# A scan kernel's last readout gives its first region beside the chain and splits its outputs on chip, and the second layer's gate is made beside the last attention

## The chip, the core and the metric

One core of a Trainium2 chip runs the whole program as one launch. The metric is the device time of one execution in microseconds (us), median of the runs shown.

## What is computed

Four layers in a row. Layer 1 is an RWKV-7 mixer over 256 context and 512 latent tokens (width 1024, 16 heads of 64): a recurrence over the tokens in two directions, a group norm of its output, a bonus term, a gate and an output projection. Layer 2 is a differential attention, layers 3 and 4 are hybrid attention layers. The change touches the end of layer 1's scan and the modulation of layer 2. Cut to that, the reference is:

```python
mod  = silu(c) @ ada_w[i] + ada_b[i]              # 3 x 1024 columns: shift, scale, gate
shift, scale, gate = split(mod)
h    = rms_norm(x, norm_g[i]) * (1 + scale) + shift
o    = scan(forward) + scan(backward)             # layer 1, per head a 64x64 state
y    = ((o - mean) * rsqrt(var + eps)) * gn_g + gn_b
y    = (y + sum(r * kd * r_k) * v) * silu(g)      # readout
x    = x + gate * (y @ w_out)
```

Every layer has this residual with a gate of its own, so the last third of the 3072 columns of `mod` is needed only where a layer's output is added back.

## The kernel before

**The scan.** Sixteen heads are worked in four pairs of feature blocks `p` (128 features `f` = 2p + j each), and the 768 tokens in three regions `R` of 256 (region 0 is the context, 1 and 2 are the latents). `Scan.chain` (L689) runs 48 steps, 12 per pair, 64 tokens of both directions each: products `ps_c` (L733), a copy to `rhs` (L740), the product with the inverted block (L768), the copy to `xz` (L771), then `ps_z` and `ps_o` (L778, L791) and the new state (L786). Each step waits for the one before on PE, ACT and DVE in turn. The four steps of a pair's first third cover region 0 in both directions, so region 0 of the last pair is complete when ten of the twelve groups of steps are done; regions 1 and 2 end only with the last step.

**The readout.** `readout(p)` (L820) takes a pair's summed outputs `osum`, subtracts the mean by a product with a block of ones (`center`, L857: L860, L861, squares L863, variance L866), takes one inverse square root over the 24 columns of the three regions (`rsqrt_dve`, 13 small DVE instructions, L72 to L76), and then for each region spreads it (L880, transposed on PE at L883, applied at L884), applies gain and bias (L889), loads two tiles `vs` from DRAM for each `j` (L853; six buffers, so three loads of two are in flight), adds two of their parts on POOL (L854), makes the bonus product (L891), and finishes with three elementwise steps (L893 to L895). The result goes to DRAM, `E.Y` (L896). For the last pair only region 0 is centred before the chain's end; all the rest waits for it.

**What follows.** The output projection needs these results as two parts, `hi` (rounded, written by ACT) and `lo` (the difference, by DVE), in tiles `act`: one pair for each group of 256 tokens, that is, for each region. `load_y` (L1134) reads `E.Y` from DRAM into `w_raw` and splits it. The object `Dense` is opened while the chain still runs (`early`, L976): blocks 0 to 5 of groups 0 and 1 are loaded, and `begin` starts the first two output blocks on them, on the first six of eight blocks. After the scan `dense` (L1818) loads blocks 6 and 7 of groups 0 and 1 and all of group 2, and `out_layer` (L1182) goes through the output blocks: 24 products each (L1079), evicted times the gate into a `yo` tile (L1212) and added to the residual (L1213), whose tiles `q_lo` and `q_hi` are loaded at L1808 and L1810.

**The modulation.** `ada` (L426) makes `mod` in pieces of 128 columns: one load of 512 KB (L432), 8 products of two columns, which the trace counts as 16 passes (L85), a copy (L87), a transpose (L90) and the bias (L96). 32 pieces run beside the chain: the gate of layer 1 (8) and all of layer 2 (24). Their buffer `ada_s` is single there, so a piece's load starts when the products of the piece before are done.

**The last attention of layer 2.** `phase_4` (L1491) runs `attention(hp)` for four pairs of heads, with a side stream that `run_streams` weaves in by counts (`NSIDE`). For the last pair the side stream has the gates and four calls of `load_y`, which bring the three earlier pairs' outputs back from DRAM. These, and the next weights, share the two buffers of `w_raw`.

**What sets the order.** The streams are woven by the numbers of the tables (`PC`, `TA`, `NSIDE` and so on); a scheduler then places the instructions of each engine, and each engine and the SP queue, which issues all DMAs, works strictly in the order it was given.

Of the kernel before, what the change touches and what calls it, by code (L numbers as in the profile page):

```python
# [205 lines left out]
class Scan:  # L206
# [3 lines left out]
    def __init__(self, E):  # L210
        self.E, self.D, self.lb = E, {}, {}
        self.ready, self.time, self.inverted, self.prepped, self.done = -1, 0.0, 0, 0, 0
        self.pend = self.pb = self.ppb = self.hop = self.pt = self.lb0 = None
        self.dones = [0] * CH
        self.read = 0
        self.ng = 0

# [601 lines left out]
    def readout(self, p):  # L819
# [47 lines left out]
            V.tensor_scalar(vc[:, R * 8:R * 8 + 8], ps[:, 0:8], 64e-5, None, OP.add)  # L867
            yield 0

        yield from center(0)  # L870
        if last:
            yield lambda: self.done >= 12
        for R in (1, 2):
            yield from center(R)
        y = rsqrt_dve(E, pool, vc, 24)
        yield 0
        for R in range(3):
            o = D["o"][R][0]
            rb = wide("rb")
            A.copy(fl(rb).rearrange("p (b v) -> p b v", v=64), y[:, R * 8:R * 8 + 8].unsqueeze(2).to_broadcast([128, 8, 64]))  # L880
            ps = psum()
            for b in range(4):
                P.transpose(ps[:, b * 128:b * 128 + 128], fl(rb)[:, b * 128:b * 128 + 128], E.ident)  # L883
            V.tensor_tensor(fl(o), fl(o), ps, OP.mult)  # L884
            yield 0
            for j in range(2):
                f = 2 * p + j
                oj, rj, pj = o[:, j, :], rb[:, j, :], ps[:, j * 256:j * 256 + 256]
                A.activation(oj, oj, AF.Identity, scale=vec(E, "gn_g", f), bias=vec(E, "gn_b", f))  # L889
                vs = streams(R, j)  # L890
                P.matmul(pj, brk[j], vs[1][:, 0], start=True, stop=True)  # L891
                yield 0
                V.tensor_tensor(rj, vs[0][:, 0], pj, OP.mult)  # L893
                (V if last and j else G).tensor_tensor(oj, oj, rj, OP.add)
                (V if last and j else G).tensor_tensor(oj, oj, vs[0][:, 1], OP.mult)  # L895
                nc.sync.dma_start(E.Y[f][:, R * 256:R * 256 + 256], oj)  # L896
                yield 0

# [39 lines left out]
CH = 1  # L940
# [3 lines left out]
def scan(E, stack):  # L944
# [2 lines left out]
    right = dict(side="right", bufs=1, reuse_waits="tile")  # L947
    left = dict(bufs=1, reuse_waits="tile")
    S = Scan(E)
    ada = [(0, m) for m in range(16, 24)] + [(1, m) for m in range(24)]  # L950
    with ExitStack() as k, ExitStack() as t, ExitStack() as a:
        kp = S.kp = k.enter_context(tc.tile_pool(name="kp", **right))
        with ExitStack() as b:
# [22 lines left out]
        def early():  # L976
            yield lambda: S.done >= 10 and S.inverted >= 6
            a.close()
            pool = stack.enter_context(tc.tile_pool(name="dn", **left))
            D.append(Dense(E, pool, stack.enter_context(tc.tile_pool(name="dn_ps", space=PSUM, **left))))  # L980
            S.pt = t.enter_context(tc.tile_pool(name="tp", **left))
            D[0].W.split(0)
            yield lambda: S.read >= 3
            D[0].load_y(E.Y, 0, 6, 2)
            if BG:
                D[0].begin(range(6))

        S.weave([x for x in rest if x in streams] + [
            [S.time + a * TC / 2, 0, S.chain(a, (0, 1) if CH == 1 else (a,)), TC, None, PC] for a in range(CH)] + [
# [499 lines left out]
def phase_4(D, hg, Y):  # L1489
# [44 lines left out]
    def attention(hp):  # L1534
# [68 lines left out]
                steps.append(tuple((lambda f=f, h=h, qb=qb: f(h, qb)) for f in (a, b, c)))  # L1603
        yield from D.pipeline(steps)

    def side(hp):
        yield from next_gates.pop()
        if hp < 3:
# [3 lines left out]
                yield next(next_gates[0])  # L1612
        else:
            ys = T["y"] = [D.group(), D.group()]
            for f in (0, 4):
                for g in range(2):
                    D.load_y(Y, f, min(f + 4, 6), g + 1, g, ys)
                    yield 0

    for _ in kqv(0):  # L1620
# [14 lines left out]
CM = 0  # L1635
OB5 = 1
GS = 0
NSIDE = (28, 8, 26, 10)
PM = 500

PW, PT4, PT5, PN = 2, 1, 1, 1
# [155 lines left out]
def dense(E, D):  # L1797
    nc, tc = E.nc, E.tc
    with tc.tile_pool(name="dm", bufs=1, reuse_waits="tile") as pool, \
            tc.tile_pool(name="dm_ps", bufs=1, space=PSUM, reuse_waits="tile") as pp:  # L1800
        D.open(pool, pp)
        D.load_y(E.Y, 6, 8, 2)
        D.load_y(E.Y, 0, 8, 3, 2)
        ys = D.ys
        cx = [pool.tile([128, 1024], FT, name="q_lo", bufs=2) for _ in range(2)]
# [124 lines left out]
```

## Time and profile before

| | us |
|---|---|
| median of 3 runs | 2320.38 |
| lowest and highest of them | 2319.94, 2320.71 |
| the profiled execution | 2326.66 |
| its span in the trace | 2324.6 |
| PE busy in it | 2106.3 (91%) |

The profiled execution is 6.28 us longer than the median, and 2.06 us of it lie outside the span. PE is busy most of the time, but the share is an average over stages: what a change in one stage is worth is read there, in the chain of waits and the timeline. "Granted clock" is the share of TensorE's full speed that it was given in a stretch: 1.0 is 2.4 GHz, 0.5 is 1.2 GHz, and values between are a mixture.

### The profile page before, as it was taken

How to read it: one execution, taken by the hardware profiler on the slowest of the kernel's cores; microseconds unless marked ns; L12 is line 12 of the kernel's file. 1: busy time of each engine (PE TensorE's matmuls, PEld its weight loads, DVE VectorE, ACT ScalarE, POOL GpSimd, SP SyncE). 2: the span in 40 equal slices, each digit the busy share in tenths (PEclk: the TensorE clock that was granted, in tenths of full speed). 3: DMA queues.
4: the chain of work that ended last, by engine and by line, in shares of the span. 5: the costliest groups of instructions: out<-in, count | busy, mean ns of one | idle time of the engine just before them, and what ended most of it. 6: DMA issues, size and time to landing. Idle time of an engine off the chain costs nothing.

```text
span 2324.6 us, 49071 instructions
## 1 busy us (share of the span) xinstructions
PE 2106.3 (91%) x18920; PEld 1867.2 (80%) x18920; DVE 1567.2 (67%) x3937; ACT 1167.2 (50%) x2634; POOL 686.0 (30%) x993
## 2 busy tenths in 40 slices
PE   7999999986899988886989999997899998999989
PEld 3989899975776776664888898987788987888878
DVE  5478868986288877723487767864676674677673
ACT  4455456563255544331255565664455564466652
POOL 0133523433036262321222223323223232032321
PEclk9999999986998788887999999998999999999999
DMA  7467456347544333153321111121312222321132
GB/s 245 136 204 227 144 188 216 105 151 230 184 135 130 90 110 101 54 181 93 134 93 55 47 58 44 42 85 48 114 64 82 67 78 91 119 80 66 60 100 82
DMA packets 190713, 263.60 MB, mean 113 GB/s; under 512 B 16145, under 2 KB 137489, under 8 KB 190353
## 3 DMA queue, kind: packets, MB, share of 16 engines
q1 hardware_dynamic: 190480, 260.48, 34.9%
q8 instruction: 149, 2.44, 0.4%
q14 instruction: 84, 0.68, 0.1%
HBM read 197.24 MB, written 63.18 MB: 112 GB/s over the span
## 4 chain that ended last, share of the span: by engine, by line
PE 47%; DVE 13%; DMA 4%; ACT 3%; issue 3%; POOL 1%; SPq 1%; ACTq 0%; DVEq 0%; POOLq 0%
PE ps_pj L1079 26%; PE ps_s L1376 3%; PE ps_m L85 2%; PE ps_t L1759 2%; PE ps_b L579 1%; PE ps_t L1586 1%; PE ps_s L1079 1%; PE ps_t L1745 1%; DMA w_raw<-in_wd_dram 1%; PE ps_t L1346 1%; DMA w_raw<-att 1%; PE ps_t L1575 1%; DVE ut L657 1%; PE ps_o L744 1%; PE ps_c L733 1%
## 5 line engine op out<-in xcount | busy, mean ns | idle before, releaser
L1079 PE MATMUL ps_pj<-w_hi,act 128*128 128x256 f32 x3264 | 645.5, 292 | 17.9 <-ACT act L1459 4.6
L1079 PEld LDWEIGHTS ps_pj<-w_hi,act 128*128 128x128 f32 x3264 | 529.5, 195 | 31.0 <-ACT act L1459 6.7
L1079 PE MATMUL ps_pj<-w_lo,act 128*128 128x256 f32 x1632 | 470.8, 289 | 0.0
L1079 PEld LDWEIGHTS ps_pj<-w_lo,act 128*128 128x128 f32 x1632 | 319.1, 196 | 0.6 <-issue 0.2
L246 PE MATMUL ps_pj<-h,b_hi 128*128 128x384 f32 (+1 forms) x1216 | 316.6, 341 | 2.7 <-ACT gh L352 1.5
L246 PEld LDWEIGHTS ps_pj<-h,b_hi 128*128 128x128 f32 x1216 | 220.0, 193 | 8.6 <-ACT gh L352 2.7
L246 PE MATMUL ps_pj<-h,b_lo 128*128 128x384 f32 (+1 forms) x608 | 206.9, 341 | 0.3 <-DVE b_lo L190 0.3
L1058 ACT CAST w_hi<-w_raw 128x1024 fp32r<-128x1024 f32 x120 | 121.0, 1050 | 58.9 <-DMA w_raw<-in_wd_dram 28.4
L1060 DVE TENSOR_TENSOR w_lo<-w_raw,w_hi 128x1024 fp32r<-128x1024 f32 x90 | 122.7, 1371 | 41.0 <-ACT w_hi L1058 40.3
L1079 PE MATMUL ps_pj<-act,w_hi 128*128 128x256 f32 x768 | 146.2, 286 | 0.0
L1735 POOL TENSOR_SCALAR p<-p,r 128x128 f32<-128x128 f32 (+2 forms) x64 | 71.8, 1122 | 239.3 <-DVE r L1729 156.7
L1060 POOL TENSOR_TENSOR w_lo<-w_raw,w_hi 128x1024 fp32r<-128x1024 f32 x30 | 72.8, 2428 | 234.3 <-ACT w_hi L1058 234.3
L579 PE MATMUL ps_b<-al,bk 64*128 64x128 f32 x768 | 127.4, 309 | 12.2 <-DVE rbk L587 10.7
L579 PEld LDWEIGHTS ps_b<-al,bk 64*128 64x128 f32 x768 | 105.7, 208 | 33.9 <-issue 21.0
L1079 PEld LDWEIGHTS ps_pj<-act,w_hi 128*128 128x128 f32 x768 | 120.9, 191 | 0.4 <-issue 0.2
L246 PEld LDWEIGHTS ps_pj<-h,b_lo 128*128 128x128 f32 x608 | 117.1, 193 | 3.6 <-issue 1.3
L547 POOL TENSOR_TENSOR s<-bk,src 64x256 f32<-64x256 f32 x96 | 76.9, 801 | 126.8 <-DVE bk L544 114.3
L1079 PE MATMUL ps_pj<-act,w_lo 128*128 128x256 f32 x384 | 109.6, 286 | 0.0
L1302 POOL TENSOR_TENSOR hx<-hx,ctab 128x256 f32<-128x256 f32 x80 | 68.0, 870 | 139.7 <-DVE ht L1300 82.5
L1565 POOL TENSOR_TENSOR p<-p 128x768 f32<-128x768 f32 x32 | 61.1, 1908 | 155.2 <-ACT p L1564 95.2
L1376 PE MATMUL ps_s<-k_s,q_hi 128*128 128x256 f32 (+2 forms) x256 | 91.2, 365 | 15.3 <-ACT p L1555 5.7
L85 PE MATMUL ps_m<-ada_s,cs 128*2 128x128 f32 x512 | 76.7, 314 | 13.4 <-DMA ada_s<-in_ada_w_dram 11.8
(323 smaller groups left out, 4920.0 us busy)
## 6 DMA issues: line engine op xcount, KB each, us to landing
w_raw<-in_wd_dram SPq DMA_DIRECT2D x120, 512.0 KB, 4.4
b_raw<-in_blocks_dram SPq DMA_DIRECT2D x84, 256.0 KB, 3.0
src<-streams SPq DMA_DIRECT2D x48, 384.0 KB, 3.6
ada_s<-in_ada_w_dram SPq DMA_DIRECT2D x32, 512.0 KB, 4.4
vs<-streams SPq DMA_DIRECT2D x48, 256.0 KB, 3.4
ada_w<-in_ada_w_dram SPq DMA_DIRECT2D x8, 1024.0 KB, 11.2
lr<-lora SPq DMA_DIRECT2D x96, 64.0 KB, 3.0
streams<-k SPq DMA_DIRECT2D x32, 192.0 KB, 2.8
```

What stands on the lines that cost most here:

```text
L85: nc.tensor.matmul(ps[0:2, 0:128 * n], E.cs[:, kb, :], w(kb), start=(kb == 0), stop=(kb == 7))
L246: E.nc.tensor.matmul(ps[gi][:, :m], w[:, kb % 4, :], h[:, kb, :], start=(n[gi] == 1), stop=(n[gi] == 24))
L547: G.tensor_tensor(v3(rev(s))[a:a + 64], ut[a:a + 64, 1 if a == 0 else 0], v3(rev(r))[a:a + 64], OP.mult)
L579: P.matmul(pb[:, c, :], bk[q:e, c].rearrange("p s t -> p (s t)"), al[q:e, c, h:3:2 - h, :], start=True, stop=True, tile_position=(q, 0))
L1058: nc.scalar.copy(hi[:, a:a + 4], raw)
L1060: e.tensor_tensor(lo[:, a:a + 4], raw, hi[:, a:a + 4], OP.subtract)
L1079: E.nc.tensor.matmul(ps, a(kb), b(kb), start=(k == 0), stop=(k == 23))
L1302: G.tensor_tensor(w4(x), w4(x), cb, OP.mult)
L1376: P.matmul(ps, q[i][:, 2 * j + h, c], k[h][:, j, a:a + n], start=(i == 0), stop=(stop and i == 1))
L1565: G.tensor_tensor(ps_[0], ps_[0], ps_[1], OP.add)
L1735: G.tensor_scalar(t, t, r[:, h:h + 1], None, OP.mult)
L1759: P.matmul(ps[h * 64:h * 64 + 64, :128], v[:, kb, o:o + 64], pt[:, h, kb, :], start=(kb == 0), stop=(kb == nk - 1), tile_position=(0, h * 64))
```

## The change

Three things, in one diff. (a) The body of the last loop of `readout` becomes `give(R, y)`. For the last pair region 0 gets an inverse square root of its own over 8 columns and is given as soon as it is centred and `Dense` has its tiles, before the wait for the chain's end; the other two regions share one over 16. (b) For the last pair regions 0 and 1 are not written to DRAM: ACT rounds them into `hi` and DVE writes the difference into `lo`, straight in the tiles of the output projection. The load of blocks 6 and 7 of groups 0 and 1 goes; region 2 still goes through DRAM. (c) The last 8 of the 24 pieces of layer 2's modulation, its gate, leave the scan. `late_gate` makes them in the side stream of the last attention, two ahead of each `load_y`, with their 512 KB in a `w_raw` buffer and their products in the bank `ps_pj`; `NSIDE` for it goes from 8 to 16.

```diff
@@ Scan.__init__
-        self.dones = [0] * CH
+        self.dones, self.next = [0] * CH, None
@@ readout
-        yield from center(0)
-        if last:
-            yield lambda: self.done >= 12
-        for R in (1, 2):
-            yield from center(R)
-        y = rsqrt_dve(E, pool, vc, 24)
-        yield 0
-        for R in range(3):
+        def give(R, y):
             o = D["o"][R][0]
...
-                nc.sync.dma_start(E.Y[f][:, R * 256:R * 256 + 256], oj)
+                if last and R < 2:
+                    hi, lo = self.next.ys[R]
+                    A.copy(hi[:, f, :], oj)
+                    V.tensor_tensor(lo[:, f, :], oj, hi[:, f, :], OP.subtract)
+                else:
+                    nc.sync.dma_start(E.Y[f][:, R * 256:R * 256 + 256], oj)
                 yield 0
+
+        yield from center(0)
+        if last:
+            y = rsqrt_dve(E, pool, vc[:, 0:8], 8)
+            yield lambda: self.next is not None and len(self.next.ys) == 2
+            yield from give(0, y)
+            yield lambda: self.done >= 12
+        for R in (1, 2):
+            yield from center(R)
+        a = 8 if last else 0
+        y = rsqrt_dve(E, pool, vc[:, a:24], 24 - a)
+        yield 0
+        for R in range(a // 8, 3):
+            yield from give(R, y[:, R * 8 - a:R * 8 + 8 - a])
@@ scan
-    ada = [(0, m) for m in range(16, 24)] + [(1, m) for m in range(24)]
+    ada = [(0, m) for m in range(16, 24)] + [(1, m) for m in range(16)]
...
+            S.next = D[0]
@@ phase_4
+    def late_gate(m):
+
+        w = D.first.tile([128, 8, 128], FT, name="w_raw", bufs=2)
+        nc.sync.dma_start(w, E.i["ada_w"][1, m // 4][:, :, m % 4 * 128:m % 4 * 128 + 128])
+        ada_bias(E, 1, m, 1, ada_columns(E, pool, D.pj, lambda kb: w[:, kb, :], 1))
@@ side
-            for f in (0, 4):
-                for g in range(2):
-                    D.load_y(Y, f, min(f + 4, 6), g + 1, g, ys)
+            for m in range(16, 24):
+                late_gate(m)
+                yield 0
+                if m % 2:
+                    f, g = divmod((m - 16) // 2, 2)
+                    D.load_y(Y, 4 * f, min(4 * f + 4, 6), g + 1, g, ys)
                     yield 0
@@
-NSIDE = (28, 8, 26, 10)
+NSIDE = (28, 16, 26, 10)
@@ dense
-        D.load_y(E.Y, 6, 8, 2)
         D.load_y(E.Y, 0, 8, 3, 2)
```

In the changed file later lines have moved: 1079 is 1092, 883 is 876, 891 is 884, 1047 is 1060, 1147 is 1160, 1173 is 1186, 1376 is 1389, 1575 is 1588, 1586 is 1599 and 1598 is 1611 there.

PE from the chain's last step (`ps_z`/`ps_o`, `ps_c`) to the first output block behind it, before. L85 and L90 are the modulation's pieces, L860 the centring of regions 1 and 2.

```order
L768 MATMUL ps_c<-rhs,lb 64x64 x8
L791 MATMUL ps_o<-rbk,xz 64x64 x8
L85 MATMUL ps_m<-ada_s,cs 2x128 x8
L860 MATMUL ps_g<-osum,bd_102 128x512
L90 MATMUL ps_m<-ident,ada_r 128x2
L85 MATMUL ps_m<-ada_s,cs 2x128 x8
L90 MATMUL ps_m<-ident,ada_r 128x2
L85 MATMUL ps_m<-ada_s,cs 2x128 x8
L90 MATMUL ps_m<-ident,ada_r 128x2
L860 MATMUL ps_m<-osum,bd_102 128x512
```

The same place in the changed program (L876 transposes region 0's inverse root, L884 is its bonus product, L1092 the first output blocks).

```order
L876 MATMUL ps_m<-ident,rb 128x128 x4
L733 MATMUL ps_c<-xz,al 64x64
L744 MATMUL ps_o<-al,xz 64x64
L733 MATMUL ps_c<-xz,al 64x64 x7
L744 MATMUL ps_o<-al,xz 64x64 x7
L884 MATMUL ps_m<-vs,brk 128x256
L768 MATMUL ps_c<-rhs,lb 64x64 x8
L884 MATMUL ps_m<-vs,brk 128x256
L791 MATMUL ps_o<-rbk,xz 64x64 x8
L1092 MATMUL ps_pj<-w_hi,act 128x256
L860 MATMUL ps_v<-osum,bd_102 128x512
```

Region 0's products now stand between those of the last step, no piece of the modulation stands behind it, and the blocks 6 and 7 of the first two output blocks stand between the centring of regions 1 and 2.

The SP queue beside the last attention of layer 2, before (L1147 brings the attention's outputs back, L1047 the next layer's weights):

```order
L1147 DMA w_raw<-att_69 128x4x256 x2
L1828 DMA q_hi<-resid 128x1024 x2
L1666 DMA v<-memv 128x512
L1388 DMA att_69<-y 128x512
L1147 DMA w_raw<-att_69 128x2x256 x2
L1047 DMA w_raw<-in_wd_dram 128x1024 x4
```

And in the changed program:

```order
L1622 DMA w_raw<-in_ada_w_dram 128x8x128 x2
L1849 DMA q_hi<-resid 128x1024 x2
L1688 DMA v<-memv 128x512
L1160 DMA w_raw<-att_69 128x4x256
L1622 DMA w_raw<-in_ada_w_dram 128x8x128
L1401 DMA att_69<-y 128x512
L1622 DMA w_raw<-in_ada_w_dram 128x8x128
L1160 DMA w_raw<-att_69 128x4x256
L1622 DMA w_raw<-in_ada_w_dram 128x8x128 x2
L1160 DMA w_raw<-att_69 128x2x256
L1622 DMA w_raw<-in_ada_w_dram 128x8x128 x2
L1160 DMA w_raw<-att_69 128x2x256
```

Eight loads have come between the four, through the same two buffers, and the next layer's weights now stand behind all twelve.

PE in that attention, changed (L1389 scores, L1588 transposes of the probabilities, L1599 their products with the values, L1611 the last transposes of a head):

```order
L90 MATMUL ps_pj<-ident,ada_r 128x2
L1588 MATMUL ps_t<-ident,p 128x128 x3
L1599 MATMUL ps_t<-v,pt 128x128 x6
L85 MATMUL ps_pj<-w_raw,cs 2x128 x8
L1588 MATMUL ps_t<-ident,p 128x128 x3
L1389 MATMUL ps_s<-k_s,q_hi 128x512
```

Each of the eight pieces stands like this among the scores and transposes of one head and of the first half of the next; the first output blocks of layer 2 (L1092), which before stood among the second head's steps, now follow the eighth piece.

## Rows read from the trace of the kernel before

**Rows 1.** The page of the profiled execution: its span.
```profile
span 2324.6 us, 49071 instructions
```

**Rows 2.** Windows of three stretches: length, busy us by engine, granted clock, DMA share, GB/s.
```profile
981.00:1056.50 75.50, 63.35 (x952) 50.01 (x944) 22.47 (x45) 24.85 (x53) 17.30 (x21) 0.86 0.50 155
1056.50:1108.50 52.00, 27.83 (x117) 18.96 (x116) 16.93 (x48) 9.18 (x18) 7.22 (x9) 0.68 0.32 98
1545.00:1615.00 70.00, 54.23 (x338) 47.16 (x336) 42.20 (x126) 41.42 (x91) 19.25 (x11) 0.85 0.19 61
```

**Rows 3.** The same windows for line 85 alone: length, PE and PEld busy, clock, DMA.
```profile
981.00:1056.50 75.50, 8.94 (x64) 5.61 (x64) 0.86 0.50 155
1056.50:1108.50 52.00, 7.39 (x48) 4.52 (x48) 0.68 0.32 98
```

**Rows 4.** Chain of waits around the end of the scan: start us, us, what ended last.
```profile
1052.53 4.22 DMA ada_s<-in_ada_w_dram
...
1065.08 4.06 DMA ada_s<-in_ada_w_dram
...
1108.47 16.64 PE ps_pj L1079 x122
```

**Rows 5.** Timeline at the last steps of the chain: start, us, instruction, idle and releaser.
```profile
1030.41 0.37 ACT L740 COPY rhs<-ps_c 128x256 f32<-128x256 f32 x1 [3.83 <-PE ps_c L733]
...
1031.92 2.88 PE L85 MATMUL ps_m<-ada_s,cs 128*2 128x128 f32 x16
...
1055.46 1.08 PE L791 MATMUL ps_o<-rbk,xz 128*64 128x64 f32 x16 [0.48 <-ACT xz L771]
...
1056.58 0.75 DVE L802 TENSOR_TENSOR osum<-osum,ps_o 128x256 f32<-128x256 f32 x2 [2.01 <-PE ps_o L791]
...
1069.27 3.57 PE L85 MATMUL ps_m<-ada_s,cs 128*2 128x128 f32 x16 [3.61 <-DMA ada_s<-in_ada_w_dram]
...
1073.76 2.08 PE L860 MATMUL ps_m<-osum,bd 128*128 128x512 f32 x2 [0.25 <-DVE mod L96]
```

**Rows 6.** Timeline of the readout and the first output blocks behind the chain.
```profile
1083.90 1.65 ACT L880 COPY rb<-rq_y 128x512 f32<-128x512 f32 x3 [6.16 <-DVE rq_y L76]
...
1088.34 0.42 DVE L893 TENSOR_TENSOR rb<-vs,ps_v 128x256 f32<-128x256 f32 x1 [0.15 <-PE ps_v L891]
...
1092.46 0.72 POOL L854 TENSOR_TENSOR vs<-vs 128x256 f32<-128x256 f32 x1 [0.42 <-DMA vs<-streams]
...
1093.24 1.22 PE L891 MATMUL ps_m<-vs,brk 128*128 128x256 f32 x2 [3.73 <-POOL vs L854]
...
1104.47 1.04 ACT L1148 CAST act<-w_raw 128x1024 fp32r<-128x1024 f32 x1 [2.34 <-DMA w_raw<-mixed]
...
1105.59 0.97 SPq L1808 DMA_DIRECT2D q_lo<-in_ctx_dram  x2
...
1110.80 1.49 POOL L1213 TENSOR_TENSOR q_lo<-q_lo,yo 128x256 f32<-128x256 f32 x1 [10.30 <-DMA q_lo<-in_ctx_dram]
...
1112.33 0.42 DVE L1212 TENSOR_TENSOR yo<-ps_pj,gt 128x256 f32<-128x256 f32 x1 [0.62 <-POOL q_lo L1213]
```

**Rows 7.** DMA issues: count, KB each, median us from issue to landing.
```profile
ada_s<-in_ada_w_dram SPq DMA_DIRECT2D x32, 512.0 KB, 4.4
vs<-streams SPq DMA_DIRECT2D x48, 256.0 KB, 3.4
...
mixed<-osum SPq DMA_DIRECT2D x24, 128.0 KB, 2.3
```

**Rows 8.** Waits of PE through the last attention of the second layer: total, times, longest.
```profile
PE ps_t L1598 <- DVE o L1595: 7.8, 3, 4.4
PE ps_s L1376 <- ACT p L1555: 5.7, 4, 2.6
```

**Rows 9.** Timeline of the SP queue beside that attention.
```profile
1535.39 1.51 SPq L1147 DMA_DIRECT2D w_raw<-att  x2
...
1566.21 11.00 SPq L1047 DMA_DIRECT2D w_raw<-in_wd_dram  x4
```

More of the change, by code (lines that the diff above doesn't have):

```diff
@@ L868, in center @@
             yield 0
-        yield from center(0)
-        if last:
-            yield lambda: self.done >= 12
-        for R in (1, 2):
-            yield from center(R)
-        y = rsqrt_dve(E, pool, vc, 24)
-        yield 0
-        for R in range(3):
+        def give(R, y):
             o = D["o"][R][0]
             rb = wide("rb")
-            A.copy(fl(rb).rearrange("p (b v) -> p b v", v=64), y[:, R * 8:R * 8 + 8].unsqueeze(2).to_broadcast([128, 8, 64]))
+            A.copy(fl(rb).rearrange("p (b v) -> p b v", v=64), y.unsqueeze(2).to_broadcast([128, 8, 64]))
             ps = psum()
```

## The prediction

> **What bounds the kernel now.** I read the granted clock and the span first, then the chain of waits, and from there the timeline of the two places that the change touches. The span is 2324.6 us [rows 1], and a change can only show where the chain of waits passes through it.
>
> The chain shows the first place at once. The scan's last product ends at 1055.46 + 1.08 = 1056.5 us [rows 5]; the first output block that the readout's results allow starts at 1108.47 and then runs 122 products without a break [rows 4]. In these 52 us PE is busy for 27.8, at a granted clock of 0.68 [rows 2]. Two things fill them. First the tail of the modulation: the chain goes through three loads of a piece, the first at 1052.53 with 4.22 us and the third at 1065.08 with 4.06 [rows 4], and its products, the last of them 3.57 us long and 3.61 us late for its load [rows 5]. Region 2's centring stands behind them on PE and starts at 1073.76, though the last sum (L802, 0.75 us from 1056.58) was ready at 1057.3 [rows 5]: 16.4 us of nothing but modulation. Then the readout itself, 1073.76 to 1108.47, 34.7 us.
>
> Inside the chain of steps the pieces also cost. One example: the copy `rhs` was ready at 1030.8, and PE went into a piece for 2.88 us from 1031.92 [rows 5], with the step's next product (L768) queued behind it. Four pieces lie in the 75.5 us before the chain's end, 8.94 us of PE [rows 3].
>
> The second place is the last attention of layer 2. From 1545 to 1615 PE is busy 54.2 of 70 us at a clock of 0.85 [rows 2], so 15.8 us are idle; 13.5 of them are waits for DVE and ACT [rows 8]. This stretch is a chain of softmax steps, not PE alone.
>
> **Part 1: behind the chain (a, b and the removal in c).** I build the new stretch from the old rows, with 0 at the chain's end.
> - The sums end at 0.8 and the centring starts at 0.9, with no piece ahead of it.
> - From the last centring's start to the spreading of the root it took 1083.90 - 1073.76 = 10.1 us [rows 5, 6]. The root over 16 instead of 24 columns is as many instructions, so this stays: 11.0.
> - From there to the first use of a bonus product it took 4.4 us with three regions to transpose [rows 6]. With two I take the first bonus product to end 3.4 after: 14.4.
> - Six `vs` buffers hold three loads of two, so region 1 and half of region 2 are there already, and the last pair of `vs` loads waits for that product. It needs 0.5 to issue and 3.4 to land [rows 7], 4.1 to be safe behind the other: 18.5 to 19. Then the addition 0.72 and the product 1.22 [rows 6]: 20.5. Everything on PE is queued behind this product.
> - Three elementwise steps of 0.42, the first cast of a reloaded tile (1.04, in a pool that opens only when the scan's tiles are read), the copy of the gate and the eviction at about 0.4 each [rows 6]: the third output block starts at 23.7. It was 51.9. The blocks ahead of it are done in the gaps.
> - What is late next: SP must first store region 2 (2.3 to land [rows 7]) and issue its reload, so the residual is asked for at about 25.1. Before, 1105.59 to 1110.80, 5.2 us, passed from its issue to its first use, and that took 1.49; the next eviction waited for it, 1112.33 [rows 6]. So the fourth block starts at 25.1 + 5.2 + 1.5 + 0.4 = 32.2; before it was 1112.33 + 0.42 - 1056.5 = 56.2.
>
> Gain 24.0 us. Region 2's reload lands at about 29 and is split by 31.5, before the fifth block, so it costs nothing; if a load were slow, PE would wait there. Bounds: 28 if the residual comes as early as the third block, 16.4 if only the modulation's tail goes. I take 24, since each step of it has its row.
>
> **Part 2: inside the chain.** Removed: four pieces, at most 8.9 us [rows 3], less where the step was waiting for ACT anyway. Added: region 0's readout, on PE one group of transposes (about 1 us) and two products of 0.6 to 1.22 [rows 6] between those of the last step, and on ACT and DVE the root, the gain, the casts and differences. If all of PE's share is exposed it is 3.4 us. The value lies between -8.9 and +3.4; I take the difference of the two, -5.
>
> **Part 3: the last attention.** Added: eight pieces. One is (7.39 - 3.57) / 2 = 1.91 us at the full clock [rows 3, 5], 15.3 in all; the small copies and additions are nothing beside 42 us of ACT and DVE [rows 2]. If all falls into the 15.8 idle us the cost is 0, if none does it is 15.3. PE works in its given order, and the idle time stands where a softmax step is late, where a piece sometimes stands and sometimes not: half, 8 us. The loads: eight more of 4.4 us [rows 7] share two buffers with four reloads. At 4.4 to land and some 2 until they are used, twelve through two buffers take 6 x 6.5 = 39 us, from 1535 to 1574 at best, where the next weights were asked for at 1566 [rows 9]. So the first output blocks of layer 2 come some 10 us later into the stretch, which is in the 8. The Trainium skill (DMA: Bandwidth & Descriptors, Rules for kernel authors) says that a load issued early and waited for late overlaps with compute; by that rule this part would be 0 and the whole sum -29. The trace does not bear it out for this code: with a single buffer each of the three last loads stood in the chain [rows 4].
>
> **Sum.** -24 - 5 + 8 = -21 us. The order of later instructions also shifts a little; no row prices that, I put 0, with 3 either way. The profiled execution takes 2326.66 us, so 2305.7 there; it is 6.3 us above the median, so the forecast is **2299.4 us**. A change of less than 0.2% (4.6 us) can't be told from none.
>
> **Rivals.**
> 1. *The cover holds.* All pieces fall into idle time, and the chain gains its full 8.9: -24 - 8.9 + 0 = -33, 2287.5 us. For it: idle time of 15.8 against 15.3. Against: PE's fixed order. Chance 0.17.
> 2. *The last attention pays in full.* 15.3 for the pieces, and the late weights add some 7 at its end, since the output blocks that filled it [rows 2] have to follow: -24 - 5 + 22 = -7, 2313 us. Chance 0.16.
> 3. *Slower.* At one place, the products of `late_gate`, PE stands for each load as it did at the scan's end, where a piece took 4.2 + 1.9 + 0.1 = 6.2 us [rows 4, 5]. Eight make 50, less 15.8 idle, +34: -24 - 5 + 34 = +5, 2325.5 us. It decides from 5.6 us a piece, (29 + 15.8) / 8. For it: SP issues in order, behind reloads that wait for casts. Against: two buffers instead of one, and some 6 us of attention between pieces. Chance 0.06.
> 4. *The clock.* A piece at 1.2 GHz took 3.57 us, at 2.4 GHz 1.91, and the slow one came after a wait of 3.6 us for a load [rows 5]. If the eight run slow, that is 13.3 more: -8, 2312.5 us. The Trainium skill (TensorE: Matmul & The Clock Gate, HAM oscillation) describes this pattern, short bursts of products between waits for loads, each burst starting at the low clock; the trace agrees in that one piece, and the two before it, 1.91 us each, speak against. Chance 0.05.
> 5. *The change does less than it says.* Region 2 still goes through DRAM and is last. If its `vs` load and reload take twice their median, the fifth block waits 6 us: -15, 2305.5 us. Chance 0.06.
>
> **How the numbers follow.** The forecast has 0.50: its own range is 2293 to 2306. The low end, 2284, takes in rival 1 and 3 us of shifts; the high end, 2315, rivals 5, 4 and most of 2. What is left out is rival 3, the worst of 2, and the best of 1. Faster by over 0.2%: the forecast, 1, 5, most of 4 and three quarters of 2, 0.87; within 0.2%: the rest of 2 and part of 3, 0.08; slower 0.05.
>
> **What would show it.** Right: no product of line 85 between the chain's last `ps_o` and the centring; the fourth output block about 32 us after the chain's end instead of 56; between the same two scores of the last attention some 8 us more, with pieces of 1.9 us and few waits for `w_raw`. Wrong: PE waiting at line 85 in the last attention for 2 us or more a piece, a granted clock there well below 0.85, or a chain whose last steps, between two products of line 768, grew beyond 8 us through region 0's readout.

## The result, and the profile after

| | median | lowest to highest | runs | to the kernel before on the same chip |
|---|---|---|---|---|
| kernel before | 2320.55 us | 2319.94 to 2326.40 | 4 | |
| changed kernel | 2301.14 us | 2296.48 to 2304.36 | 4 | 0.9895 (0.9866 to 0.9923) |

The forecast was 2299.4 us, the range 2284 to 2315. The profiled execution took 2302.14 us (forecast for it: 2305.7). The page gives its span, against 2324.6 before [rows 1]:

```profile
span 2300.3 us, 49070 instructions
```

The windows of the changed kernel that answer to [rows 2]: the last 75.5 us of the chain, the stretch from the chain's end (1045.2) to the third output block (1070.45), and the last attention of layer 2 from the same point of the work as before. Columns as there.

```profile
969.70:1045.20 75.50, 64.39 (x1037) 53.39 (x1035) 28.58 (x59) 25.77 (x53) 19.79 (x23) 0.78 0.45 137
1045.20:1070.45 25.25, 14.23 (x56) 9.75 (x56) 14.50 (x44) 7.39 (x14) 5.10 (x7) 0.62 0.25 70
1508.50:1587.16 78.66, 67.70 (x497) 56.84 (x496) 45.38 (x135) 45.52 (x101) 18.74 (x11) 0.96 0.37 116
```

The same windows for line 85 alone, which answer to [rows 3]:

```profile
969.70:1045.20 75.50, 0.00 (x0) 0.00 (x0) 0.78 0.45 137
1045.20:1070.45 25.25, 0.00 (x0) 0.00 (x0) 0.62 0.25 70
1508.50:1587.16 78.66, 17.26 (x128) 10.63 (x128) 0.96 0.37 116
```

The modulation has left the scan, and the 52 us of [rows 2] behind the chain have become 25.25. In the last attention the products of line 85 add 17.3 us on PE, yet PE is busy only 13.5 us more than in the window of before (67.7 for 54.2, and that window runs on 1.8 us past the last head). Its granted clock there stands at 0.96 where it was 0.85.

The timeline of the changed kernel on both sides of the scan's end, and at the one late piece that PE waited for:

```profile
1044.19 1.00 PE L791 MATMUL ps_o<-rbk,xz 128*64 128x64 f32 x16
...
1045.87 1.08 PE L860 MATMUL ps_v<-osum,bd 128*128 128x512 f32 x2
...
1054.68 1.14 ACT L873 COPY rb<-rq_y 128x512 f32<-128x512 f32 x2 [4.61 <-DVE rq_y L76]
...
1058.57 1.23 SPq L853 DMA_DIRECT2D vs<-streams  x2
...
1063.69 1.22 PE L884 MATMUL ps_g<-vs,brk 128*128 128x256 f32 x2 [3.35 <-POOL vs L854]
...
1067.60 1.23 DVE L1162 TENSOR_TENSOR act<-w_raw,act 128x1024 fp32r<-128x1024 f32 x1 [0.64 <-ACT act L1161]
...
1069.07 1.22 PE L1186 MATMUL ps_t<-yo,ones 128*128 128x128 f32 x4 [1.10 <-DVE yo L1185]
...
1070.45 0.58 PE L1092 MATMUL ps_pj<-w_hi,act 128*128 128x256 f32 x1 [0.16 <-DVE yo L1225]
...
1075.24 0.42 DVE L1225 TENSOR_TENSOR yo<-ps_pj,gt 128x256 f32<-128x256 f32 x1 [0.63 <-POOL q_lo L1226]
...
1521.95 0.55 SPq L1622 DMA_DIRECT2D w_raw<-in_ada_w_dram  x1
...
1526.97 3.57 PE L85 MATMUL ps_pj<-w_raw,cs 128*2 128x128 f32 x16 [2.82 <-DMA w_raw<-in_ada_w_dram]
...
1558.02 9.28 SPq L1060 DMA_DIRECT2D w_raw<-in_wd_dram  x4
```

**One profile isn't enough here.** Before the first place that the change touches, the two kernels give PE the same instructions in the same order until about 945 us. Yet the first profiles already stand 5.6 us apart there, and the three profiles of the changed kernel, from one chip to another, 17. It goes with the granted clock. These are the windows from the start to the last eleven steps of the chain, of the first profile of before, and of the first and the third of the changed kernel:

```profile
0.00:955.53 955.53, 876.54 (x8651) 738.75 (x8651) 697.36 (x1582) 467.92 (x983) 331.97 (x676) 0.91 0.51 160
```

```profile
0.00:949.91 949.91, 866.32 (x8655) 730.76 (x8657) 698.21 (x1585) 467.38 (x983) 336.36 (x678) 0.92 0.51 161
```

```profile
0.00:967.37 967.37, 888.25 (x8651) 747.03 (x8651) 700.22 (x1588) 467.89 (x983) 336.02 (x682) 0.89 0.50 158
```

DVE, ACT and POOL are busy as long in each, within some us; PE's time goes from 866 to 888 us as its clock falls from 0.92 to 0.89. So 0.2%, which I had called what a measurement can tell, was too fine: beside the experiments the runs of the kernel before spread from 2314 to 2344 us. What follows is therefore read by stretches, between points of the work that every profile has: the first score of layer 2 (L1376, now L1389) and the transposition of its last head (L1598, now L1611). Two profiles of before and three of the changed kernel give:

| stretch, us | before | changed | difference of the means | forecast |
|---|---|---|---|---|
| start to the chain's last eleven steps | 955.5, 958.6 | 949.9, 951.6, 967.4 | -0.8 | 0 |
| last eleven steps of the chain | 101.0, 101.5 | 95.3, 90.7, 90.9 | -9.0 | -5 |
| chain's end to the first score | 196.1, 197.8 | 170.9, 169.7, 169.9 | -26.8 | -24 |
| first score to the last head | 360.6, 363.5 | 371.1, 367.8, 371.8 | +8.2 | +8 |
| last head to the end | 708.2, 714.9 | 709.8, 706.5, 708.6 | -3.2 | 0, with 3 either way |

The boundary between the first two rows is read to within 0.4 us, and the end is that of PE's last product, some 3.2 us before the end of the span. The five differences add up to -31.6 us, more than the medians give below (19 to 27): both profiles of before were longer than their kernel's median, by 6.1 and 12.5 us, while those of the changed kernel lie on both sides of theirs (+1.0, -13.6, +11.9). The first pair of profiles alone gives -5.6, -5.7, -25.2, +10.5 and +1.6, and its first -5.6 lie ahead of the change.

### The profile page after: what moved, and what is told of

Read it like the earlier page. It is cut to its first block, busy times and chain, and to the rows that moved or that the text cites. A ratio compares the mean times of both kernels' runs of the same rounds, so it can differ in the third digit from the quotient of the medians.

```text
span 2300.3 us, 49070 instructions
## 1 busy us (share of the span) xinstructions
PE 2093.5 (91%) x18914; PEld 1861.9 (81%) x18920; DVE 1574.1 (68%) x3952; ACT 1167.7 (51%) x2636; POOL 688.1 (30%) x993
## 4 chain that ended last, share of the span: by engine, by line
PE 45%; DVE 13%; DMA 5%; ACT 4%; issue 3%; POOL 2%; SPq 0%; ACTq 0%; DVEq 0%; POOLq 0%
PE ps_pj L1092 25%; PE ps_s L1389 3%; DMA w_raw<-in_wd_dram 2%; PE ps_t L1781 2%; PE ps_t L1599 2%; PE ps_b L579 1%; PE ps_s L1092 1%; PE ps_t L1767 1%; PE ps_m L85 1%; DMA w_raw<-att 1%; DVE hx L1303 1%; DVE w_lo L1073 1%; PE ps_t L1359 1%; PE ps_t L1588 1%; DVE al L556 1%
## 5 line engine op out<-in xcount | busy, mean ns | idle before, releaser
L1092 PE MATMUL ps_pj<-w_hi,act 128*128 128x256 f32 x3264 | 646.3, 292 | 22.0 <-ACT act L1472 4.8
L1092 PEld LDWEIGHTS ps_pj<-w_hi,act 128*128 128x128 f32 x3264 | 530.6, 196 | 36.0 <-ACT act L1472 7.0
L1092 PE MATMUL ps_pj<-w_lo,act 128*128 128x256 f32 x1632 | 472.7, 290 | 0.0
L1092 PEld LDWEIGHTS ps_pj<-w_lo,act 128*128 128x128 f32 x1632 | 320.0, 196 | 1.2 <-issue 0.9
L1092 PE MATMUL ps_pj<-act,w_hi 128*128 128x256 f32 x768 | 145.7, 285 | 0.0
L1092 PEld LDWEIGHTS ps_pj<-act,w_hi 128*128 128x128 f32 x768 | 120.7, 191 | 0.4 <-issue 0.2
L1092 PE MATMUL ps_pj<-act,w_lo 128*128 128x256 f32 x384 | 109.7, 286 | 0.0
L1389 PE MATMUL ps_s<-k_s,q_hi 128*128 128x256 f32 (+2 forms) x256 | 88.5, 355 | 9.8 <-ACT p L1748 5.9
L189 ACT CAST b_hi<-b_raw 128x512 fp32r<-128x512 f32 x84 | 52.1, 622 | 71.1 <-PE ps_pj L246 56.6
```

Source lines behind the costliest of these rows:

```text
L189: nc.scalar.copy(hi, raw)
L1092: E.nc.tensor.matmul(ps, a(kb), b(kb), start=(k == 0), stop=(k == 23))
L1389: P.matmul(ps, q[i][:, 2 * j + h, c], k[h][:, j, a:a + n], start=(i == 0), stop=(stop and i == 1))
```

## The experiments

The experiments ran on three chips, on each beside the kernel before. On the first chip were the readout's edits alone, the gate's move alone, the split undone and the eight stream buffers (before: 2325.43 us, 25 runs); on the second the changed kernel again, the eighth of the products, the products twice and the third buffer (2329.53 us, 11 runs); on the third both kernels again, the smaller loads and the undone split again (2328.37 us, 17 runs). Ratios are to the kernel before on the same chip; stretches are from each run's one profile.

### Controls: both kernels again

No edit.

> The kernel before itself, for a second profile of it: a ratio of 1.00. From layer 2's first score to the transposition of its last head it took 360.6 us in the first profile, the kernel with the gate kept in the scan 366.6 and the changed one 371.1 and 367.8. If the first profile stood for the kernel, 360 to 362 us again; rival (the granted clock in the waits of the softmax steps moves it by some us from run to run, as it moved the untouched scan by 6): 364 to 368 us, and the price of the late gate is then 4 to 6 us and not 8 to 10.

> The changed kernel itself, as a control on the chip of the next three runs: 0.9895 of the kernel before if the first figure holds (0.9866 to 0.9923). In its profile I expect the stretch from the chain's end to the first score of layer 2 at 171 us (before: 196), and the last attention with its pieces 8 to 11 us longer than before; whatever differs from the first profile in stretches that the change doesn't touch is the clock's drift from run to run.

> The changed kernel, as the control of this chip: 0.9895 to 0.990 of the kernel before; 367 to 371 us from the first score of layer 2 to its last head.

Measured: before again 0.9999 (0.9971 to 1.0027), the changed kernel 0.9900 (0.9862 to 0.9938) and 0.9884 (0.9843 to 0.9924), medians 2305.03 and 2301.84 us. With the first result the gain is 1.0 to 1.2% three times, 19 to 27 us by the medians. The stretches are in the table. The first score to the last head of before came to 363.5, between the two expected ranges and just under the rival's, and the last attention is 8.2 us longer by the means. The changed kernel's 367.8 there is 7.2 us above the first profile of before, less than the 8 to 11 I expected, and its 371.8 lies just above the 367 to 371.

### The readout's edits alone

The gate goes back into the scan, into the places it had:

```diff
-    ada = [(0, m) for m in range(16, 24)] + [(1, m) for m in range(16)]
+    ada = [(0, m) for m in range(16, 24)] + [(1, m) for m in range(24)]
...
-NSIDE = (28, 16, 26, 10)
+NSIDE = (28, 8, 26, 10)
```

and `side` loads as before, without `late_gate`.

> The readout's two edits alone, the gate left in the scan. My sum (the modulation's tail and the last pair's pieces are a term of their own, the last attention's price too): the tail's 16.4 us and some 5 us of pieces in the chain come back, the 10.5 us that the last attention grew by go: about 2301 + 21 - 10.5 = 2312 us, 8 to 9 us under the kernel before. Rival (the readout beside the chain is the whole gain, the tail was only filling time in which the readout waited anyway): 2301 - 10.5 = 2291 us.

Measured: 2308.01 us, 0.9922 (0.9894 to 0.9951); 2312 us would be 0.9963 of the 2320.5 it was set against, 2291 us 0.9873, so it lies between. The chain's last eleven steps took 99.7 us, so some 7 of the 9 us saved there came back. The chain's end to the first score took 175.4, where 196.1 and 197.8 stood before: the readout alone is worth 22 us there (197.0 - 175.4), and only 5 of the 16.4 came back. The windows of line 85 on both sides of this run's chain end (1052.2) show that the products are all there again:

```profile
976.70:1052.20 75.50, 8.95 (x64) 5.62 (x64) 0.86 0.52 162
1052.20:1083.92 31.72, 7.39 (x48) 4.49 (x48) 0.84 0.31 94
```

Its timeline shows why they cost so little: the centring and the two regions' transpositions now stand between the pieces, and the loads of the pieces arrive while the readout goes on.

```profile
1054.38 1.13 PE L860 MATMUL ps_v<-osum,bd 128*128 128x512 f32 x2
...
1063.47 3.57 PE L85 MATMUL ps_m<-ada_s,cs 128*2 128x128 f32 x16 [1.06 <-DVE rb L886]
...
1071.46 1.91 PE L85 MATMUL ps_m<-ada_s,cs 128*2 128x128 f32 x16 [0.73 <-DMA ada_s<-in_ada_w_dram]
```

The longest wait for a piece's load here is 0.73 us, where it was 3.61 [rows 5]. Both theories fall as stated: the tail is neither 16.4 us on its own nor nothing.

### The gate's move alone

The readout stays as it was in the kernel before:

```diff
-    ada = [(0, m) for m in range(16, 24)] + [(1, m) for m in range(24)]
+    ada = [(0, m) for m in range(16, 24)] + [(1, m) for m in range(16)]
...
+            for m in range(16, 24):
+                late_gate(m)
+                yield 0
...
-NSIDE = (28, 8, 26, 10)
+NSIDE = (28, 16, 26, 10)
```

> The kernel before with the gate's move alone. My sum: -16.4 behind the chain, up to -8.9 inside it (no readout of region 0 is put there), +10.5 to +13 in the last attention: 2320.5 - 16.4 - 7 + 11.5 = 2308.5 us. Rival (the move gives back in the attention all that it takes from the scan): 2318 to 2321 us. Second rival (the move is the whole change, the on-chip readout hides nothing): 2301 us.

Measured: 2310.29 us, 0.9933 (0.9905 to 0.9960); my sum, 2308.5 of 2320.5, is 0.9948. The first rival, 0.999 and more, is out; the second, 2301 us or 0.9916, lies in the interval too, and only the stretches speak against it. The last eleven steps took 91.5 us, the chain's end to the first score 179.8 (17 us less than before, for 16.4 forecast), the first score to the last head 372.5 (+10.5). The windows of the chain's last steps and of the stretch to the third block:

```profile
1046.17:1080.66 34.49, 18.05 (x65) 13.22 (x65) 16.52 (x45) 8.51 (x15) 6.90 (x9) 0.67 0.40 117
955.00:1046.17 91.17, 71.19 (x1308) 59.96 (x1304) 38.87 (x85) 33.32 (x63) 21.91 (x36) 0.79 0.35 108
```

The third block starts 34.5 us after the chain's end. Together with the run before this is the step that matters for part 1: the gate alone saves 17 us there, the readout alone 22, both together 27, and not 39. Each edit takes away a part of the time in which the other's work could hide.

### The on-chip split undone

```diff
-                if last and R < 2:
-                    hi, lo = self.next.ys[R]
-                    A.copy(hi[:, f, :], oj)
-                    V.tensor_tensor(lo[:, f, :], oj, hi[:, f, :], OP.subtract)
-                else:
-                    nc.sync.dma_start(E.Y[f][:, R * 256:R * 256 + 256], oj)
+                nc.sync.dma_start(E.Y[f][:, R * 256:R * 256 + 256], oj)
...
+        D.load_y(E.Y, 6, 8, 2)
         D.load_y(E.Y, 0, 8, 3, 2)
```

> The changed kernel with region 0's early readout and the moved gate, but regions 0 and 1 stored and loaded again. If the trip through DRAM was on the path: a store of 2.3 us and a load of 3.4 us with a cast stand between the last product of region 1 and the first output block that needs all of it, so 5 to 8 us slower, 2306 to 2309 us. Rival (PE waits for the last scan streams anyway, until 18.5 us after the chain's end, and the trip is hidden behind that wait): 2301 us.

> The run without the split on chip once more, beside the changed kernel on one chip. Its stretch from the chain's end to layer 2's first score was 176.7 us against 170.9 and 169.7, yet its median stood at 0.9866 of the kernel before. By the stretch, 5 to 7 us slower than the changed kernel: 0.992. Rival (something later in it is faster by 10 us, as its last 600 us were in the first profile): 0.987 again, and the last stretch at 606 us again.

Measured: 2292.39 us, 0.9866 (0.9831 to 0.9901), and beside the changed kernel on one chip 2295.34 us, 0.9853 (0.9816 to 0.9890; the changed kernel there: 2301.84 and 0.9884). In its place the trip through DRAM costs what was expected: the third block starts 30.0 and 28.8 us after the chain's end instead of 24.3 to 25.3, and the first score comes after 176.7 and 176.3 us, 6.4 later than with the split. But the kernel isn't slower. From the first score of layer 3 to the end it takes 606.2 and 606.0 us where the changed kernel took 612.9, 610.8 and 612.3. The windows of that last stretch, of the third profile of the changed kernel and of the repeat:

```profile
1696.37:2308.62 612.25, 573.42 (x4592) 520.47 (x4596) 403.41 (x1104) 340.65 (x858) 161.74 (x140) 0.98 0.25 81
```

```profile
1690.37:2296.39 606.02, 571.41 (x4592) 520.16 (x4596) 399.93 (x1104) 340.90 (x858) 163.45 (x140) 0.98 0.25 82
```

The same work, the same clock, PE busy 2.0 us less and idle 4.2 us less. What differs is the order of the instructions, which shifts there with an edit 650 us earlier. I forecast 5 to 8 us slower and then 5 to 7, and was wrong in the total both times; what came is the rival of the second expectation. Which of the shifted instructions does it was not tried.

### Eight stream buffers

```diff
-                vs = [self.pt.tile([128, 2, 256], FT, name="vs", bufs=2 * TV) for _ in range(2)]
+                vs = [self.pt.tile([128, 2, 256], FT, name="vs", bufs=2 * TV + 2) for _ in range(2)]
```

> The changed kernel with eight stream buffers in the last readout instead of six, so that region 2's last loads needn't wait for region 1's product. In the changed kernel PE stood 3.35 us for them at 1063.69 us with all output blocks queued behind. If that wait is on the path: 3 to 5 us faster, 2296.5 to 2298 us, and the third output block about 21 us after the chain's end instead of 25.3. Rival (the pool of the next stage, which opens when the scan's tiles are free, or the loads' own place in SP's queue holds the block just as long): 2301 us.

Measured: 2310.00 us, 0.9937 (0.9914 to 0.9961): not faster. The wait is gone, as the timeline shows, and the third block starts 1063.60 - 1041.15 = 22.5 us after the chain's end instead of 24.3 to 25.3:

```profile
1054.90 0.69 PE L884 MATMUL ps_m<-vs,brk 128*128 128x256 f32 x2
1055.68 0.67 PE L884 MATMUL ps_g<-vs,brk 128*128 128x256 f32 x2
1059.98 1.23 PE L1186 MATMUL ps_t<-yo,ones 128*128 128x128 f32 x4 [3.63 <-DVE yo L1185]
...
1063.60 0.58 PE L1092 MATMUL ps_pj<-w_hi,act 128*128 128x256 f32 x1 [0.16 <-DVE yo L1225]
```

The wait for `yo` grew to 3.63 us in its place. By the first score nothing was left: 170.7 us against 169.7 to 170.9. So the first theory had the block nearly right (22.5 for 21), and the rival had the gain by the first score right, which is none. The first score to the last head then took 375.3 us, 5 more than the changed kernel. The order has shifted here too; what makes this kernel longer than either expectation is open.

### One eighth of the late products

```diff
-    for kb in range(8):
+    for kb in range(kbs):
...
-        ada_bias(E, 1, m, 1, ada_columns(E, pool, D.pj, lambda kb: w[:, kb, :], 1))
+        ada_bias(E, 1, m, 1, ada_columns(E, pool, D.pj, lambda kb: w[:, kb, :], 1, 1))
```

with 8 as the default of `kbs` in `ada_columns`, the last product ending the sum, and every load as it was.

> The changed kernel with the eight loads of the late gate kept, but only one of the eight sections of each piece's product computed (seven eighths of the sum of the last gate are left out). If the price of the last attention is PE time, the pieces fall from 1.91 to 0.24 us each and PE has 13 us less to do: some 8 us faster than the changed kernel, 0.986 of the kernel before. Rival (the price is the loads: waits for buffers, reloads and next weights that come late): at most 3 us faster, 0.9885.

Measured: 2298.59 us, 0.9881 (0.9855 to 0.9908). The interval holds both 0.986 and 0.9885, so the total decides nothing. From the first score to the last head 371.5 us: as long as with all products (370.2 by the mean of three). From the transposition of the sixth of the eight heads to that of the last, the windows of the changed kernel, and of this run:

```profile
1521.85:1587.16 65.31, 54.35 (x392) 45.25 (x392) 36.21 (x104) 38.28 (x86) 18.61 (x11) 0.95 0.38 117
```

```profile
1518.16:1585.44 67.28, 48.73 (x307) 41.18 (x307) 37.90 (x106) 37.76 (x84) 19.20 (x11) 0.87 0.36 113
```

PE executes 85 products fewer, but is busy only 5.6 us less, since its clock falls from 0.95 to 0.87, and what it saves turns into idle time: 18.6 instead of 11.0 us. In this run PE's waits there are:

```profile
PE ps_s L1389 <- ACT p L1568: 6.2, 2, 4.6
PE ps_t L1611 <- DVE o L1608: 4.6, 2, 4.4
PE ps_pj L85 <- DMA w_raw<-in_ada_w_dram: 4.6, 4, 1.6
```

So with the loads whole, the stretch isn't shorter for seven eighths of the products less: there they lie in cover. The rival, loads, is left standing with 4.6 us of waits.

### The loads cut too

```diff
-        w = D.first.tile([128, 8, 128], FT, name="w_raw", bufs=2)
+        w = D.first.tile([128, 8, 128], FT, name="w_raw", bufs=2)[:, 0:1, :]
-        nc.sync.dma_start(w, E.i["ada_w"][1, m // 4][:, :, m % 4 * 128:m % 4 * 128 + 128])
+        nc.sync.dma_start(w, E.i["ada_w"][1, m // 4][:, 0:1, m % 4 * 128:m % 4 * 128 + 128])
```

on top of the run above.

> As the run with one eighth of the products, and only the eighth of each load that they read is loaded (64 instead of 512 KB; the same seven eighths of the last gate's sum are left out). With an eighth of the products the last attention stayed as long as with all of them: PE's idle time grew and its clock fell. If the loads are what holds it (PE waited 4.2 us for them, and they share two buffers with the reloads): 4 to 6 us less than with whole loads, 365 to 367 us from the first score to the last head, 0.986 of the kernel before. Rival (the softmax steps and the clock set the stretch whatever is put beside it): 370 to 372 us again, 0.988.

Measured: 2291.68 us, 0.9846 (0.9807 to 0.9886), and 366.2 us from the first score to the last head, 5.2 less than with whole loads: inside the 365 to 367 of the first theory. The same window and the waits for loads in it:

```profile
1517.78:1578.80 61.02, 47.54 (x306) 40.22 (x305) 37.27 (x103) 36.72 (x84) 18.82 (x11) 0.87 0.25 79
```

```profile
PE ps_t L1611 <- DVE o L1608: 6.4, 2, 4.4
PE ps_s L1389 <- ACT p L1568: 2.7, 2, 2.4
...
PE ps_pj L85 <- DMA w_raw<-in_ada_w_dram: 0.9, 2, 0.7
```

PE has nearly the same to do at the same clock; its idle time fell from 18.6 to 13.5 us. The waits at line 85 fell by 3.7 us. The softmax waits moved too, one from 6.2 down to 2.7 and one from 4.6 up to 6.4. So with the products cut, whole loads cost this stretch some 5 us; my account of it is PE's fixed order, in which a piece whose load is late keeps the next scores behind it. This rests on one profile each, where three of the changed kernel differ by 4.0 us, and small loads under whole products were not run: how the price divides in the changed kernel is not shown.

### The products twice

```diff
-        ada_bias(E, 1, m, 1, ada_columns(E, pool, D.pj, lambda kb: w[:, kb, :], 1))
+        for _ in range(2):
+            ada_bias(E, 1, m, 1, ada_columns(E, pool, D.pj, lambda kb: w[:, kb, :], 1))
```

> The changed kernel with each late piece's product, copy, transposition and addition made twice. If PE is the bound of the last attention with the pieces in it (in the changed kernel 72.7 of 83.65 us busy), eight more products of 1.91 us cost 8 x 1.91 = 15.3 us less what little idle time is left: 10 to 15 us slower than the changed kernel, 0.995 of the kernel before. Rival (the pieces lie in idle time, the cost is the loads): 0 to 4 us slower, 0.990.

Measured: 2303.44 us, 0.9899 (0.9866 to 0.9931). In the total no difference to the changed kernel can be told (0.9900), with intervals of 8 us either way, and the forecast of 0.995 lies outside. In the stretch it is there: 380.1 us from the first score to the last head, 9.9 more than the changed kernel. The same window:

```profile
1512.99:1587.36 74.37, 67.64 (x529) 54.92 (x528) 34.51 (x112) 40.13 (x94) 18.69 (x11) 0.99 0.35 110
```

Now PE is busy 67.6 of 74.4 us at a clock of 0.99. The first eight pieces filled most of what cover there was; of the 13.6 us that the second set takes in this window (27.1 for 13.5, by line 85's rows), 9.1 lengthen it.

### A third buffer

```diff
-        w = D.first.tile([128, 8, 128], FT, name="w_raw", bufs=2)
+        w = (pool.tile([128, 8, 128], FT, name="w_ada") if m % 2 else
+             D.first.tile([128, 8, 128], FT, name="w_raw", bufs=2))
```

> The changed kernel with a third buffer, of its own, for every other late load. In the changed kernel PE stood 2.82 us at the third piece, whose load could be asked for only when the second piece was done, and that piece then took 3.57 instead of 1.91 us. If two buffers cost that: 4 to 5 us faster than the changed kernel, 0.9875 of the kernel before. Rival (the next softmax step is late by then, and waits instead): no difference, 0.9895.

Measured: 2295.37 us, 0.9871 (0.9840 to 0.9901). No wait for a late load is left among PE's waits, but the stretch stays at 372.4 us; a softmax step is waited for instead, which the changed kernel didn't have at this length:

```profile
PE ps_t L1611 <- DVE o L1608: 5.1, 2, 4.4
PE ps_s L1389 <- ACT p L1568: 4.3, 1, 4.3
```

In the stretch the rival is right: under whole products, taking away the waits for loads gained nothing. The total's 0.9871 meets the 0.9875 of the first theory, but not by its mechanism. It is lower through the end again, 604.0 us from layer 3's first score, as in the run without the split. This kernel and that one have the lowest medians of those that compute the whole gate; that either beats the changed one is not shown, since the intervals overlap.

## Why the prediction was right

The time (2301.1 for 2299.4) and the signs of its three parts came out. That the time came within 2 us is partly luck: in the two controls the changed kernel gained 24.5 and 26.5 us by the medians, and two of the three parts were forecast too small. Its steps one by one:

**Behind the chain: -24 forecast, -26.8 measured.** The built stretch held almost step by step. From the chain's end, forecast and first profile: centring 0.9 and 0.7; spreading of the root 11.0 and 9.5; the first bonus product's end 14.4 and 13.4; the end of the product that waits for the last `vs` loads 20.5 and 19.7. The third block was to start at 23.7 and started at 25.3. Two steps that I left out account for that: DVE's split of region 2's first reload, 1.23 us, which stands ahead of the second gate's scaling on DVE, and the products that spread that gate on PE, 1.22 us from 1069.07, for which the eviction waits. The other error worked the other way: I measured the gain at the fourth block, whose eviction does wait for the residual (30.1 us after the chain's end, to 30.5; forecast 32.2), and took 24 for it. But PE never stood for that eviction, neither now nor before, where its 122 products ran without a break [rows 4]. The gain is that of the third block, 51.92 - 25.25 = 26.7, near the bound of 28 that I had put aside. That the tail alone gives 16.4 is confirmed by the move alone (17), though these 16.4 us were not all modulation: region 1's centring, 1.12 us, stands among them.

**Inside the chain: -5 forecast, -9.0 measured.** The mis-sized term is this one, and both of its bounds were off (their sum, -8.9 + 3.4, is -5.5 besides). Five pieces left the eleven steps and not four: I had counted the last 75.5 us only. Line 85 in the eleven steps of before:

```profile
955.53:1056.54 101.01, 10.70 (x79) 6.71 (x78) 0.85 0.40 124
```

The move alone brought these steps from 101.3, the mean of before, to 91.5, so 9.8 us of the pieces' 10.7 (11.9 in the second profile of before) were in the way. Region 0's readout, which I charged with up to 3.4 us, cost nothing that can be told: 90.7 and 90.9 with it. The first profile's 95.3 isn't its doing. The excess lies in the first five of the eleven steps, at a lower clock, and region 0's transposition stands in the last but one (1040.00 in that profile). The first profile and the second, split at the start of the sixth step:

```profile
949.74:1011.18 61.44, 49.51 (x792) 42.32 (x793) 32.32 (x78) 23.24 (x40) 11.34 (x26) 0.64 0.33 100
1011.18:1045.19 34.01, 29.11 (x532) 24.04 (x530) 12.59 (x26) 11.83 (x27) 12.56 (x14) 0.95 0.44 132
```

```profile
951.23:1008.20 56.97, 41.62 (x791) 35.05 (x792) 32.12 (x78) 22.91 (x40) 10.74 (x23) 0.79 0.35 108
1008.20:1042.31 34.11, 31.33 (x532) 25.93 (x530) 12.53 (x26) 11.92 (x27) 12.47 (x14) 0.85 0.44 132
```

**The last attention: +8 forecast, +8.2 measured, for the wrong reason.** I had half of the pieces' 15.3 us fall into idle time and half be paid. In the runs an eighth of the products left the stretch as long (371.5 for 370.2 us), and small loads on top of that took 5.2 off it. The rest, some 4 us over before, stays with loads and products cut to an eighth. The run that keeps the whole gate in the scan has it too: 366.6 us, without a late piece or its small steps. The last two heads of before, and of that run, with a wait in it that stood at 0.6 us in before:

```profile
1557.30:1613.21 55.91, 43.36 (x264) 37.39 (x265) 33.36 (x94) 33.32 (x75) 18.88 (x11) 0.83 0.22 71
```

```profile
1533.58:1594.15 60.57, 43.29 (x264) 38.34 (x265) 34.92 (x96) 33.77 (x76) 18.77 (x11) 0.82 0.19 66
```

```profile
PE ps_t L1588 <- POOL p L1578: 4.3, 3, 1.8
```

So these 4 us point to the order of the instructions, which the readout's edits shift here, and not to the late gate; beside that run the gate itself costs 3.6 us (370.2 - 366.6). Beside before, the move alone costs 10.5. With one profile of each, the price of the late gate is known only as lying between. In a sentence beside this term stood a rule of the Trainium skill (DMA: Bandwidth & Descriptors, Rules for kernel authors), by which a load issued early and waited for late overlaps with compute. In the first profile PE waited for one of the eight late loads, and that one was not early: it was issued at 1521.95, when the piece before had left the buffer, and PE stood for it 2.82 us until 1526.97. The other seven were not waited for, as the rule has it.

**The shift of later instructions: 0 with 3 either way, -3.2 measured**, which can't be told from 0, since the two profiles of before differ by 6.7 there. In two other kernels the stretch from layer 3 on is 6 and 8 us shorter than the changed kernel's mean. That is larger than I gave it.

**The rivals.** Of the first, the chain's full gain came true, and the products' cover as far as the run with an eighth of them shows it, but the last attention's longer time stayed. The second and third didn't come: the longest wait for a late load was 2.8 us, once (2.3 and 2.1 in the other profiles), and the next weights were asked for at 1558.0, 8 us earlier than before by the clock and 28 later in the work, without a wait of PE for them in the stretch. The fourth is seen in one piece of eight: 3.57 us, behind that wait of 2.82; the others took 1.9. Region 2's reload held nothing up.

## What to carry to other kernels

Two edits that empty the same stretch need not add: each had been partly hidden behind the other's time, 17 and 22 us alone were 27 together. Work moved into the idle time of a chain of short steps can be nearly free as far as the gaps reach (here one set of products, while a second set cost 9.9 us), but its loads can cost where its products don't: count how many buffers they share, with whom, and which instruction is queued behind a late one. Before a price is read off two kernels, look for a run that has their shifted order without the work that is priced. And before a profile's stretches are compared, compare one that the change can't have touched; here it differed by as much as the effect.

## What was not expected of the hardware

More products made the rest of the products faster. In the last attention PE's granted clock was 0.83 without the pieces, 0.87 with an eighth of them, 0.95 with all and 0.99 with twice as many. So part of what a piece costs is given back by its neighbours: in the windows shown the 85 products left out had taken 11.0 us by line 85's own rows (13.5 against 2.5), and leaving them out saved 5.6 us of PE time, and none of the stretch.

The scan's time also varies with the clock: nearly the same instructions took 943 to 967 us up to the chain's last eleven steps in fourteen profiles, the shortest at a granted clock of 0.93, the longest at 0.89. The first four runs of before, within 0.3% of each other, gave no hint of that.
